# HGRN scores of levels 1 to 16 as 32-column tiles in one burst, and attention bursts in another order, in an inference step of a two-layer decoder

## The chip, the cores and the metric

One core of a Trainium2 chip runs the whole step. The metric is the device time of one execution in microseconds (us): 2629.91 before the change, the median of three runs (2628.09 to 2630.24).

## What is computed

The reference runs two groups of tokens through the same weights: a prompt of 256 tokens and 8 samples of 4 tokens, 288 columns in all. Layer 0 is an HGRN2 recurrence with 16 heads, layer 1 a sliding-window attention with sinks; each is followed by a SwiGLU FFN, and every sublayer stands between two RMS norms. What the change touches is the recurrence and the attention:

```
def step(S, inp):                      # gla_chunked, per head, float32
    qc, kc, vc, gc = inp
    b = jnp.cumsum(gc, axis=1)
    o_inter = jnp.einsum('bthk,bhkv->bthv', qc * jnp.exp(b), S)
    diff = b[:, :, None] - b[:, None, :]
    decay = jnp.exp(jnp.where(tril[None, :, :, None, None], diff, -jnp.inf))
    scores = jnp.einsum('bthk,bshk,btshk->btsh', qc, kc, decay)
    o_intra = jnp.einsum('btsh,bshv->bthv', scores, vc)
    b_last = b[:, -1]
    S_new = jnp.exp(b_last)[..., None] * S + jnp.einsum(
        'bshk,bshv->bhkv', kc * jnp.exp(b_last[:, None] - b), vc)
    return S_new, o_inter + o_intra
```

A score between a query at t and a key at s carries the product of the forget gates f between them, per element of the head's 128 dimensions. In the attention every query head takes the softmax of its scores over at most 128 keys and a sink, and multiplies the values.

## The kernel before

**Projections and ticks.** Activations lie transposed, 128 features by 288 tokens. `project` multiplies them by a weight matrix in steps of 128 rows. Weights come from memory as `raw`; ACT rounds them to `hi` (L219), DVE makes the rest `lo` (L220), and TensorE does three passes per block (`hi` and `lo` on the high part of the input, `hi` on the low part) into four accumulators of a tick: 12 passes of 288 columns. After each tick the function `tick` (L183) lets every launched generator run to its next `yield`. So a generator's matmuls stand between two ticks of a projection, in the order written; PE and ACT keep this order, DVE's is set by a scheduler. Everything small on PE shares three PSUM banks (`small`, L134).

**One HGRN head.** While head n + 1 is projected (16 ticks), the generator `recurrence` (L631) works on head n. It computes the decays in seven levels: at level B = 1, 2, 4, ... 64 a key in the first half of a block of 2B tokens meets the queries in the second half (the second 128 tokens run backwards, so there the halves change roles). Both have been multiplied by the gates up to the block's middle. Products of gates per block are in `Ts` (tile `tt`, L646).

- Step 1 starts the load of the sample state `s0` and makes `tt` and `qf` = q times f (L649). Four steps later comes the burst: scores of each token with itself and of the samples' own tokens, and the samples' queries with the state, all as tiles of 32 columns (L129 with `k`, `ksm`, `qsm`, `s0`).
- Then one step per level (`level`, L731): ACT merges the keys of both token halves into `km` (L678), DVE scales the keys (L705), PE multiplies 128 by 128, DVE scales the queries (L741) and copies the scores under a mask into `scp` (L742).
- Meanwhile values are transposed (L721, L722), spread per sample into `vb` (L748), the state is decayed into `sn` (L655). Then `state` (L778) adds the samples' new state, `ss` is stored, keys are transposed (L792), and the last steps make the output `po` and the prompt's final state.

After every second head, `gate_norm` (L578) normalizes two heads' outputs, in every second step, beside the next head's recurrence; its logarithm and exponential need another table on ACT (L300).

**Attention.** `prompt_heads` (L976) handles two heads ("par" 0 and 1, in rows 0 to 63 and 64 to 127 of the operands) in steps: scores (two banks), softmax, transposes (L996), values (L129 with `pt`, `vtok`). `sample_heads` (L1016) does the samples' eight sequences: four score bursts (par by half of the sequences; `kk`, `qs`, `kc`), one per tick, then four pairs of transposes (L1049, L1050) and four value bursts (`vnew`, `vc`).

**Fills.** Where a post-norm keeps PE from its next operand, `fill_time` (L142) runs 26, 24 and 19 matmuls of several shapes whose results nobody reads.

Of the kernel before, what the change touches and what calls it, by code (L numbers as in the profile page):

```python
# [11 lines left out]
F32 = mybir.dt.float32  # L12
F32R = mybir.dt.float32r
# [5 lines left out]
P = 128  # L19
# [19 lines left out]
NL = len(LEVELS)  # L39
FFN_PARTS = (16, 16, 12)  # L40
# [6 lines left out]
REC_DELAY = 4  # L47
# [67 lines left out]
def trunk(tc, I, O):  # L115
# [26 lines left out]
    def fill_time(kind, x):  # L142
        ps = small()
        y = strided(x, 0, [(1, 512)])
        b = y.bitcast(BF16)
        for n, rows, cols, src in (
            ((6, P, P, y), (6, P, TS, x), (4, P, P, x.rearrange("p (a b) -> p a b", a=2)), (6, P, P, x[:, :TP]), (4, P, P, x[:, :144])),
            ((6, 64, P, x), (6, P, 64, x), (6, P, P, strided(x, 0, [(2, NT)])), (6, P, P, strided(x, 2 * NT, [(1, NT)]))),
            ((8, P, P, b[:, :NT]), (6, P, P, b[:, :512]), (3, P, P, x.bitcast(F32))),
        )[kind]:  # L150
            out = ps[:cols, :src.free_size()] if len(src.shape) == 2 else ps[:cols, :NT].rearrange("p (a b) -> p a b", a=2)
            w = y.bitcast(src.dtype)[:rows, :cols]
            for _ in range(n):
                mm(out, w, src[:rows], True, True)

# [41 lines left out]
    fills = [0, 1, 2]  # L197
# [220 lines left out]
    def partial(pick, n, mix, first, norm=None, gcol=None, fill=None):  # L418
        add = None

        def each(m, acc):
# [7 lines left out]
            if m < 2:  # L429
                add = norm.square_one(dst)  # L430
                if m == 0:
                    gain(mix, gcol, 12)
            elif m == 2:
                norm.keep(dst)
            else:
                norm.flush(SPLIT)
                if fill is not None:
                    fill(PRE0)
                norm.tail(dst)
                if fill is not None:  # L440
                    fill(PRE1)
                else:
                    fill_time(fills.pop(0), pick(0)[0])
# [100 lines left out]
    with tc.tile_pool(name="hg", bufs=2) as hg:  # L544
        lmask = hg.tile([P, NL, P], U8, name="lmask", bufs=1)
# [3 lines left out]
        bmask = hg.tile([P, NB], F32, name="bmask", bufs=1)  # L549
        scores, scores_s = [], []  # L550
        for z in range(2):
            t = hg.tile([P, 2 * P], F32, name=f"sc{z}", bufs=1)
            nc.gpsimd.memset(t, 0.0)
            scores.append(t)
            t = hg.tile([P, TS], F32, name=f"scs{z}", bufs=1)
            nc.gpsimd.memset(t, 0.0)
            scores_s.append(t)

        def constants():
            wide = hg.tile([P, (NL + 1) * P + TS], mybir.dt.int32, tag="vb", name="wide", bufs=1)  # L560
# [6 lines left out]
            nc.vector.tensor_copy(lmask, wide[:, :NL * P].rearrange("p (l c) -> p l c", l=NL))  # L567
            yield
            nc.vector.tensor_copy(imask, wide[:TS, (NL + 1) * P:])
            nc.vector.tensor_copy(second, wide[:, NL * P:(NL + 1) * P])  # L570
# [41 lines left out]
        def evacuate(hd, accs, r):  # L612
            fg = hg.tile([P, NT], F32, tag="fg", name="fg", bufs=QB)
            q = hg.tile([P, NT], F32, tag="q", name="q", bufs=QB)
            gs = hg.tile([P, NT], F32, tag="gs", name="gs", bufs=3)
            k = hg.tile([P, NT], F32, tag="k", name="k", bufs=QB)
            v, s, s2 = work("v"), work("s"), work("s2")
# [9 lines left out]
            nc.vector.tensor_scalar(k, fg, -1.0, 1.0, op0=ALU.mult, op1=ALU.add)  # L627
            nc.vector.tensor_mul(gs, gs, s2)
            return q, fg, k, v, gs

        def recurrence(hd, delay, q, fg, k, v, gs):  # L631
            scp, scs = scores[hd % 2], scores_s[hd % 2]
            blk = scp.rearrange("p (a c) -> p a c", a=2)
            s0 = hg.tile([P, NB, P], F32, tag="s0", name="s0", bufs=1)
            (nc.gpsimd if hd else nc.sync).dma_start(s0, I["s0"][hd])
            rv = hg.tile([P, 4, TS], F32, tag="rep", name="rep", bufs=QB)
            nc.scalar.copy(rv, v[:, TP:NT].unsqueeze(1).broadcast_to([P, 4, TS]))
# [3 lines left out]
            for B in LEVELS:  # L641
# [6 lines left out]
            qf = hg.tile([P, NT], F32, tag="qf", name="qf", bufs=1)  # L648
            nc.vector.tensor_mul(qf, q, fg)  # L649
            t4 = Ts[2][:, 64:72]  # L650
            sn = hg.tile([P, NB, P], F32, tag="sn", name="sn", bufs=1)

            def decay(*bs):
                for b in bs:
                    nc.scalar.activation(sn[:, b, :], s0[:, b, :], AF.Identity, scale=t4[:, b:b + 1])  # L655

            yield
            ksm = hg.tile([P, 2, TS], F32, tag="ksm", name="ksm", bufs=1)
            qsm = hg.tile([P, 2, TS // 2], F32, tag="qsm", name="qsm", bufs=1)
            k2, q2 = [z[:, TP:NT].rearrange("p (j two) -> p j two", two=2) for z in (k, qf)]  # L660
            k4, q4 = [z[:, TP:NT].rearrange("p (j two b) -> p j two b", two=2, b=2) for z in (k, qf)]
            T1 = fg[:, TP:NT].rearrange("p (j two) -> p j two", two=2)
            T2 = Ts[1][:, P:P + TS // 2].rearrange("p (j two) -> p j two", two=2)
            nc.scalar.copy(ksm[:, 0, :], k[:, TP:NT])
            nc.scalar.copy(qsm[:, 0, :], q2[:, :, 1])
            nc.vector.tensor_mul(k2[:, :, 0], k2[:, :, 0], T1[:, :, 1])
            nc.vector.tensor_mul(q2[:, :, 1], q2[:, :, 1], T1[:, :, 0])
            nc.scalar.copy(ksm[:, 1, :], k[:, TP:NT])
            nc.scalar.copy(qsm[:, 1, :].rearrange("p (j b) -> p j b", b=2), q4[:, :, 1, :])
            nc.vector.tensor_mul(k4[:, :, 0, :], k4[:, :, 0, :], T2[:, :, 1:2].broadcast_to([P, NB, 2]))  # L670
            nc.vector.tensor_mul(q4[:, :, 1, :], q4[:, :, 1, :], T2[:, :, 0:1].broadcast_to([P, NB, 2]))

            kms = []

            def merge_k(li):
                B = LEVELS[li]
                km = hg.tile([P, P], F32, tag="km", name="km")
                nc.scalar.copy(km.rearrange("p (j s b) -> p j s b", s=2, b=B), strided(k, 0, [(2 * B, P // (2 * B)), (P + B, 2), (1, B)]))  # L678
                kms.append(km)

            for _ in range(delay - 1):
                yield
            merge_k(0)
            ps = small()
            for t in range(2):
                for g in range(4):
                    a = slice(t * P + g * TS, t * P + g * TS + TS)
                    mm(ps[TS * g:TS * (g + 1), t * TS:(t + 1) * TS], k[:, a], q[:, a], True, True)
            mm(ps[:TS, 2 * TS:3 * TS], ksm[:, 0, :], q[:, TP:NT], True, True)
            mm(ps[:TS, 3 * TS:3 * TS + 16], ksm[:, 0, :], qsm[:, 0, :], True, True)  # L690
            mm(ps[:TS, 3 * TS + 16:4 * TS], ksm[:, 1, :], qsm[:, 1, :], True, True)
            q = qf
            past = small()
            for g in range(4):
                mm(past[TS * g:TS * (g + 1), :2 * P].rearrange("p (b c) -> p b c", b=2), q[:, TP:NT], s0[:, 2 * g:2 * g + 2, :], True, True)
            own = hg.tile([P, 2, TS], F32, tag="own", name="own", bufs=1)
# [540 lines left out]
```

## Time and profile before

| | |
|---|---|
| three runs | 2628.09, 2629.91, 2630.24 us |
| the profiled execution | 2627.88 us |
| its span in the profile | 2626.1 us |
| granted clock of TensorE | 1.00 over the span |
| busy: PE, DVE, ACT | 2606.5, 1591.7, 1259.8 us |
| HGRN stage | up to about 550 us of the span |
| attention stage | about 1553 to 1700 us |

PE is TensorE's matmuls, PEld its weight loads, DVE VectorE, ACT ScalarE. A matmul of float32 operands appears as two passes, one of rounded operands as one. An instruction's duration reaches into the next one's: the distance from start to start says what it costs.

### The profile page before, as it was taken

To read this page: it belongs to the slowest core of one execution; us is meant where nothing else is said; L and a number is where in the kernel's file an instruction comes from. 1 tells how busy PE (TensorE), PEld (TensorE's weight loads), DVE (VectorE), ACT (ScalarE), POOL (GpSimd) and SP (SyncE) were. 2 spreads that over 40 slices of the span, in tenths; PEclk is the share of its full clock that TensorE was granted. 3 is DMA by queue.
4 is the path that set the end of the run, shared out by engine and by line. 5 is a ranking of instruction groups with operands and counts; after the bars stand their busy time and mean duration, and the time that the engine had idled before them with its cause. 6 is when DMAs were issued, how large, how long until landed. Compare 5 with 4: busy or idle time off the path is not lost.

```text
span 2626.1 us, 48851 instructions
## 1 busy us (share of the span) xinstructions
PE 2606.5 (99%) x20057; PEld 2565.5 (98%) x20058; DVE 1591.7 (61%) x2939; ACT 1259.8 (48%) x2217; POOL 34.2 (1%) x70
## 2 busy tenths in 40 slices
PE   9999999999999999999999999999999999999999
PEld 9999999999999999999999998899999999999998
DVE  8888888867654345544455787658544354544555
ACT  6666666655433334333334566656333343333343
POOL 0000000000000000000000000000000000000000
PEclk9999999999999999999999999999999999999999
DMA  6555555554545555455555553345455555555553
GB/s 225 178 167 168 163 165 169 165 161 148 180 155 178 166 169 163 159 177 166 164 166 169 165 158 105 99 159 166 156 178 166 166 165 161 175 165 167 162 161 123
DMA packets 119007, 428.03 MB, mean 163 GB/s; under 512 B 13792, under 2 KB 14112, under 8 KB 118784
## 3 DMA queue, kind: packets, MB, share of 16 engines
q1 hardware_dynamic: 112752, 404.49, 48.1%
q0 software_dynamic: 6032, 20.42, 2.3%
q8 instruction: 157, 2.57, 0.4%
q14 instruction: 66, 0.54, 0.1%
HBM read 412.74 MB, written 12.12 MB: 162 GB/s over the span
## 4 chain that ended last, share of the span: by engine, by line
PE 92%; DVE 5%; ACT 2%; issue 1%; DMA 0%; SPq 0%; DVEq 0%; ACTq 0%
PE acc L129 87%; PE pm L129 4%; DVE lo L220 1%; ACT hi L219 1%; DVE sc L742 1%; DVE qf L741 0%; DVE vb L748 0%; DVE k L705 0%; PE pm L996 0%; ACT y L594 0%; DMA raw<-w_in_in 0%; DVE v L760 0%; DVE mix L1129 0%; DVE yl L585 0%; ACT y L596 0%
## 5 line engine op out<-in xcount | busy, mean ns | idle before, releaser
L129 PE MATMUL acc<-xa,hi 128*128 128x288 f32 x12160 | 2476.5, 296 | 0.8 <-ACT xa L293 0.4
L129 PEld LDWEIGHTS acc<-xa,hi 128*128 128x128 f32 x12160 | 1971.5, 189 | 16.5 <-issue 14.2
L129 PE MATMUL acc<-xa,lo 128*128 128x288 f32 x6080 | 1791.6, 296 | 0.9 <-DVE lo L220 0.9
L220 DVE TENSOR_TENSOR lo<-raw,hi 128x1024 fp32r<-128x1024 f32 x759 | 919.0, 1224 | 747.7 <-ACT hi L219 746.9
L129 PEld LDWEIGHTS acc<-xa,lo 128*128 128x128 f32 x6080 | 1141.7, 188 | 2.0 <-DVE lo L220 1.1
L219 ACT CAST hi<-raw 128x1024 fp32r<-128x1024 f32 x759 | 784.1, 1048 | 715.8 <-PE acc L129 485.6
L474 ACT ACTIVATE f<-f 128x288 f32<-128x288 f32 x88 | 39.2, 445 | 203.9 <-DVE f L473 203.9
L473 DVE TENSOR_TENSOR f<-acc,rpre 128x288 f32<-128x288 f32 x84 | 38.4, 458 | 113.9 <-PE acc L129 113.9
L678 ACT COPY km<-k 128x128 f32<-128x128 f32 x112 | 34.8, 310 | 47.3 <-PE pm L129 23.8
L129 PE MATMUL pm<-qf,km 128*128 128x128 f32 x224 | 47.1, 292 | 8.6 <-ACT km L678 6.0
L293 ACT ACTIVATE xa<-h,gains 128x288 fp32r<-128x288 f32 x80 | 38.8, 527 | 31.8 <-DVE h L410 25.2
L129 PEld LDWEIGHTS pm<-qf,km 128*128 128x128 f32 x224 | 35.1, 189 | 13.4 <-ACT km L678 9.8
L742 DVE COPY_PREDICATED sc<-lmask,pm 128x128 f32<-128x128 uint8 x112 | 42.7, 381 | 0.9
L334 DVE TENSOR_TENSOR ss<-ss,sq 128x576 f32<-128x576 f32 x48 | 36.3, 757 | 10.3 <-ACT sq L333 8.6
L483 ACT CAST xa<-f 128x288 fp32r<-128x288 f32 x88 | 35.4, 434 | 14.0 <-DVE f L482 13.8
L655 ACT ACTIVATE sn<-s,tt 128x128 f32<-128x128 f32 x128 | 40.9, 392 | 0.0
L296 DVE SCALAR_TENSOR_TENSOR xa<-h,gains,xa 128x288 fp32r<-128x288 f32 x80 | 40.1, 517 | 0.4 <-ACT xa L293 0.4
L487 DVE TENSOR_TENSOR xa<-f,xa 128x288 fp32r<-128x288 f32 x88 | 36.6, 456 | 5.7
L741 DVE TENSOR_TENSOR qf<-qf,tt 128x128 f32<-128x128 f32 x96 | 27.7, 288 | 20.3 <-PE pm L129 19.9
L476 DVE TENSOR_TENSOR f<-acc,rpre 128x288 f32<-128x288 f32 x84 | 38.4, 457 | 0.0
L482 DVE TENSOR_TENSOR f<-f,f 128x288 f32<-128x288 f32 x88 | 36.1, 451 | 0.1
L452 DVE TENSOR_TENSOR mix<-acc,mix 128x288 f32<-128x288 f32 x56 | 22.2, 453 | 16.6 <-PE acc L129 16.6
(264 smaller groups left out, 1235.2 us busy)
## 6 DMA issues: line engine op xcount, KB each, us to landing
raw<-w_gu_in SPq DMA_DIRECT2D x352, 512.0 KB, 3.5
raw<-w_dn_in SPq DMA_DIRECT2D x176, 512.0 KB, 3.5
raw<-w_in_in SPq DMA_DIRECT2D x127, 512.0 KB, 3.6
raw<-w_oh_in SPq DMA_DIRECT2D x32, 512.0 KB, 3.7
raw<-w_q_in SPq DMA_DIRECT2D x32, 512.0 KB, 3.5
raw<-w_oa_in SPq DMA_DIRECT2D x32, 512.0 KB, 3.5
ss_out<-sn POOLq DMA_DIRECT2D x16, 512.0 KB, 6.1
s<-s_in POOLq DMA_DIRECT2D x15, 512.0 KB, 5.6
```

The costliest lines, as they stand in the source:

```text
L129: nc.tensor.matmul(out, lhsT, rhs, start=start, stop=stop, skip_group_check=True)
L219: nc.scalar.copy(hi, raw)
L220: lows.append(lambda: nc.vector.tensor_sub(lo, raw, hi.bitcast(F32)))
L293: nc.scalar.activation(xh, h[:, kt, :], AF.Identity, scale=g)
L296: nc.vector.scalar_tensor_tensor(xl, h[:, kt, :], g, xh.bitcast(F32), op0=ALU.mult, op1=ALU.subtract)
L334: return lambda: nc.vector.tensor_add(self.ss, self.ss, sq)
L473: nc.vector.tensor_mul(t1, accs[2 * a], r)
L474: nc.scalar.activation(t1, t1, AF.Silu)
L476: nc.vector.tensor_mul(t2, accs[2 * a + 1], r)
L487: nc.vector.tensor_sub(al, t2s[a], ah.bitcast(F32))
L655: nc.scalar.activation(sn[:, b, :], s0[:, b, :], AF.Identity, scale=t4[:, b:b + 1])
L742: nc.vector.copy_predicated(strided(scp, B, [(2 * B, n), (P - B, 2), (1, B)]), lmask[:, li].rearrange("p (j s b) -> p j s b", s=2, b=B), p ...
```

## The change

- Each head's keys and queries (after q times f) live in one tile `kq`, so that one DVE multiplication scales both for both token halves (`scale`). `pair` makes one level of `Ts` at a time.
- For levels 1 to 16 ACT keeps a merged copy of keys (`km`) and queries (`qm`) ahead of each scaling (`merge`). The scores of these five levels become 20 matmuls with 32 columns of keys and 32 of queries, in the one burst, which now comes at the ninth step. DVE copies them under five masks into `cs` (128 x 64) and multiplies `cs` out into `scp`. Levels 32 and 64 keep a full matmul each, one per step (`wide_scores`), and their copy comes a step later (`put`).
- The values' transposes come three steps before the burst, the keys' one step before. Three copies of the samples' keys and values go into the state's matmul in place of four. The state is decayed in place in `s0`. A head has 15 steps, it had 16.
- Prompt heads: the value matmuls of the two halves alternate. Sample heads: both halves of a score burst and of a value burst in one step; `vnew` and `pnew` have 128 rows, with zeros.
- `warm(30, ...)`, 30 matmuls of 288 columns, stands in place of `fill_time`.

```diff
+LOW = 5
+KQ = 4 * P + 2 * TS
-REC_DELAY = 4
+REC_DELAY = 2
...
-                    fill_time(fills.pop(0), pick(0)[0])
+                    warm(WARM, pick(0)[0])
...
+            def merge(li):
+                B = LEVELS[li]
+                km = hg.tile([P, P], F32, tag="km", name="km", bufs=LOW + 1)
+                nc.scalar.copy(km.rearrange("p (j s b) -> p j s b", s=2, b=B), strided(kq, 0, [(2 * B, P // (2 * B)), (3 * P + B, 2), (1, B)]))
+                kms.append(km)
+                if li < LOW:
+                    qm = hg.tile([P, P], F32, tag="qm", name="qm", bufs=LOW)
+                    nc.scalar.copy(qm.rearrange("p (s j b) -> p s j b", s=2, b=B), queries(li))
+                    qms.append(qm)
+            def scale(li):
+                B = LEVELS[li]
+                nc.vector.tensor_mul(halves(li), halves(li), strided(Ts[li], 1, [(-1, 2), (2, P // B), (0, B)]))
...
+            def wide_scores(li):
+                B = LEVELS[li]
+                n = P // (2 * B)
+                ps = small()
+                mm(ps[:, :P].rearrange("p (s j b) -> p s j b", s=2, b=B), kms.pop(0), queries(li), True, True)
+                scale(li)
...
+            merge(0)
+            yield
+            pair()
+            scale(0)
+            sample_scale(0)
+            merge(1)
+            yield
...
+            yield
+            pair()
+            scale(3)
+            merge(4)
+            yield
+            pair()
+            scale(4)
+            merge(5)
...
+            for li in range(LOW):
+                km, qm = kms.pop(0), qms.pop(0)
+                for g in range(4):
+                    a = slice(TS * g, TS * (g + 1))
+                    mm(ps[a, (2 + li) * TS:(3 + li) * TS].rearrange("p (s c) -> p s c", s=2), km[:, a], strided(qm, TS * g // 2, [(P // 2, 2), (1, TS // 2)]), True, True)
...
+            pair()
+            put = wide_scores(LOW)
+            merge(NL - 1)
+            nc.vector.tensor_tensor(scp.rearrange("p (t g c) -> p t g c", t=2, g=4), cs.unsqueeze(2).broadcast_to([P, 2, 4, TS]),
...
-            for par in range(2):
-                rows = slice(64 * par, 64 * par + 64)
-                hc = (2 * pair + par) * HD
-                mm(po[rows, :P], vtok[:, 0, hc:hc + HD], pt[:, par, 0, :], True, True)
-                mm(po[rows, P:TP], vtok[:, 1, hc:hc + HD], pt[:, par, 1, :], False, False)
-                mm(po[rows, P:TP], vtok[:, 2, hc:hc + HD], pt[:, par, 2, :], False, True)
+            for z in range(3):
+                for par in range(2):
+                    rows = slice(64 * par, 64 * par + 64)
+                    hc = (2 * pair + par) * HD
+                    mm(po[rows, P * (z > 0):P * (z > 0) + P], vtok[:, z, hc:hc + HD], pt[:, par, z, :], z == 0, z != 1)
...
+            for hb in range(2):
+                pss = [small() for _ in range(2)]
+                for ps, rows in zip(pss, halves):
+                    mm(ps[:, new[hb]], qv[rows, hb * P:(hb + 1) * P], kk[rows, pair, 3 * P:], True, True)
+                for bq in range(4):
+                    b = 4 * hb + bq
+                    for ps, rows in zip(pss, halves):
+                        mm(ps[32 * bq:32 * bq + 32, old[hb]], qv[rows, 32 * b:32 * b + 32], kc[rows, b, :], False, True)
...
+                for par, rows in enumerate(halves):
+                    hc = (2 * pair + par) * HD
+                    mm(po[rows, hb * P:(hb + 1) * P], vnew[:, hc:hc + HD], pnew[:, par * P:(par + 1) * P], hb == 0, False)
+                for bq in range(4):
+                    b = 4 * hb + bq
+                    for par, rows in enumerate(halves):
+                        mm(po[rows, 32 * b:32 * b + 32], vc[:, b, par * HD:(par + 1) * HD], pt[:, par * P + 32 * bq:par * P + 32 * bq + 32], False, True)
```

**PE, one HGRN head from the burst on, in a head with a gate norm.** Before (`pm` is a PSUM tile; `k`, `q` keys and queries, `s` the sample state, `km` merged keys; the projection's rows lie between, left out as "..."):

```order
L129 MATMUL pm<-q,k 32x32 [waits DVE_49]
L129 MATMUL pm<-q,k 32x32 x7
L129 MATMUL pm<-q,ksm 32x32 [waits Activation_49]
L129 MATMUL pm<-qsm,ksm 32x16 [waits Activation_49] x2
L129 MATMUL pm<-s_2232,qf 32x256 [waits DMASW1_49,DVE_49,PE_49]
L129 MATMUL pm<-s_2232,qf 32x256 x3
...
L721 MATMUL pm<-ident,v 128x128 x2
L722 MATMUL pm<-ident,rep 128x128
L129 MATMUL pm<-qf,km 128x128 [waits DVE_49]
```

and with the change:

```order
L132 MATMUL pm<-q,k_2260 32x32 [waits DVE_49]
L132 MATMUL pm<-q,k_2260 32x32 x7
L132 MATMUL pm<-qm,km 32x32 x16
L132 MATMUL pm<-qm,km 32x32 [waits Activation_49]
L132 MATMUL pm<-qm,km 32x32 x3
L132 MATMUL pm<-q,few 32x32
L132 MATMUL pm<-few 32x16 x2
L132 MATMUL pm<-s_2252,kq 32x256 [waits DMASW2_49,DVE_49]
L132 MATMUL pm<-s_2252,kq 32x256 x3
...
L132 MATMUL pm<-kq,km 128x128 [waits DVE_49]
...
L132 MATMUL pm<-kq,km 128x128 [waits Activation_49]
```

The 20 matmuls with `qm` have come into the burst. Behind it seven ticks held a level each (of the before one is shown); two are left, and the second waits for ACT's merge.

**DVE, from the burst to the scaling of level 32 and 64, in a head without a gate norm.** Before, per level (`sc` is `scp`):

```order
L705 TENSOR_TENSOR k<-k,tt 128x2x32x2 [waits Activation_49]
L741 TENSOR_TENSOR qf<-qf,tt 128x2x32x2 [waits PE_49]
L742 COPY_PREDICATED sc_120<-lmask,pm 128x32x2x2
L705 TENSOR_TENSOR k<-k,tt 128x2x16x4 [waits Activation_49]
L741 TENSOR_TENSOR qf<-qf,tt 128x2x16x4 [waits PE_49]
```

and with the change:

```order
L765 TENSOR_TENSOR cs<-pm,eyes 128x64 [waits PE_49]
L769 COPY_PREDICATED cs<-lmask,pm 128x2x16 [waits DVE_49]
L769 COPY_PREDICATED cs<-lmask,pm 128x2x8x2 [waits DVE_49]
L779 COPY_PREDICATED every<-second,pm 128x128 [waits Activation_49]
L769 COPY_PREDICATED cs<-lmask,pm 128x2x4x4 [waits DVE_49]
L769 COPY_PREDICATED cs<-lmask,pm 128x2x2x8 [waits DVE_49]
L772 COPY_PREDICATED scs<-imask,pm 32x32
L784 TENSOR_TENSOR scp<-cs,bmask 128x256 [waits DVE_49]
L673 TENSOR_TENSOR kq<-kq,tt 128x2x4x32 [waits PE_49]
L692 COPY_PREDICATED scp<-wmask,pm 128x2x2x32
L673 TENSOR_TENSOR kq<-kq,tt 128x2x2x64 [waits PE_49]
```

Three operations per level have become one scaling (L673), which for levels 1 to 16 stands ahead of the burst; the copies of the burst's scores now stand ahead of the scaling of level 32.

**PE, a score burst of the samples beside a prompt head's scores.** Before:

```order
L129 MATMUL pm<-kk,q 128x128 [waits DVE_49,PE_49]
L129 MATMUL pm<-kk,q 128x256
L129 MATMUL pm<-kk,qs 128x32 [waits DVE_49,Activation_49]
L129 MATMUL pm<-kc,qs 32x128 [waits DMASW7_49]
L129 MATMUL pm<-kc,qs 32x128 x3
```

and with the change:

```order
L132 MATMUL pm<-kk,q 128x128 [waits DVE_49,PE_49]
L132 MATMUL pm<-kk,q 128x256
L132 MATMUL pm<-kk,qs 128x32 [waits DVE_49,Activation_49]
L132 MATMUL pm<-kk,qs 128x32 [waits DVE_49]
L132 MATMUL pm<-kc,qs 32x128 [waits DMASW7_49]
L132 MATMUL pm<-kc,qs 32x128 x7
```

The burst holds both halves and waits twice for DVE, once per PSUM bank.

## Rows read from the trace of the kernel before

**Rows 1.** The page, busy time and share; and the chain by engine:

```profile
PE 2606.5 (99%) x20057; PEld 2565.5 (98%) x20058; DVE 1591.7 (61%) x2939; ACT 1259.8 (48%) x2217; POOL 34.2 (1%) x70
...
PE 92%; DVE 5%; ACT 2%; issue 1%; DMA 0%; SPq 0%; DVEq 0%; ACTq 0%
```

**Rows 2.** Windows: stretch, length, PE, PEld, DVE, ACT, POOL busy, clock, DMA, GB/s:

```profile
700.00:1300.00 600.00, 600.00 (x4540) 600.00 (x4540) 285.59 (x333) 226.36 (x269) 0.00 (x0) 1.00 0.52 166
104.75:137.58 32.83, 31.85 (x262) 30.70 (x261) 29.45 (x77) 23.18 (x52) 1.61 (x3) 1.00 0.47 160
137.58:168.89 31.31, 31.07 (x259) 30.16 (x258) 23.96 (x65) 17.05 (x42) 1.61 (x3) 1.00 0.55 175
```

**Rows 3.** Timeline of PE, one head: start, length in us, line, operands, count:

```profile
201.67 0.33 PE L129 MATMUL pm<-q,k 128*32 128x32 f32 x16
201.82 0.23 PE L129 MATMUL pm<-q,ksm 128*32 128x32 f32 x2
...
202.01 0.60 PE L129 MATMUL pm<-s,qf 128*32 128x256 f32 x5
202.54 0.40 PE L129 MATMUL acc<-xa,hi 128*128 128x288 f32 x1
...
208.36 0.38 PE L129 MATMUL pm<-qf,km 128*128 128x128 f32 x2
...
210.17 0.39 PE L129 MATMUL pm<-qf,km 128*128 128x128 f32 x2
...
212.37 0.46 PE L129 MATMUL pm<-qf,km 128*128 128x128 f32 x2 [0.24 <-DVE qf L741]
```

**Rows 4.** The chain in a head with a gate norm: start, length, engine:

```profile
111.81 0.45 ACT L300
...
114.03 0.68 ACT y L596
...
115.15 0.49 PE pm L129 x2
```

**Rows 5.** Groups of instructions: busy us, mean ns of one, idle before:

```profile
L220 DVE TENSOR_TENSOR lo<-raw,hi 128x1024 fp32r<-128x1024 f32 x759 | 919.0, 1224 | 747.7 <-ACT hi L219 746.9
...
L678 ACT COPY km<-k 128x128 f32<-128x128 f32 x112 | 34.8, 310 | 47.3 <-PE pm L129 23.8 <-DVE k L705 23.5
...
L649 DVE TENSOR_TENSOR qf<-q,fg 128x288 f32<-128x288 f32 x16 | 7.3, 455 | 0.0
```

**Rows 6.** Timeline of DVE, the evacuation ahead of that burst:

```profile
194.82 0.45 DVE L618 TENSOR_TENSOR q<-acc,rpre 128x288 f32<-128x288 f32 x1
...
197.72 0.31 DVE L627 TENSOR_SCALAR k<-fg 128x288 f32<-128x288 f32 x1
```

**Rows 7.** Timeline of PE in the attention stage:

```profile
1570.54 1.15 PE L129 MATMUL pm<-pt,vtok 128*64 128x128 f32 x12
...
1575.43 0.93 PE L129 MATMUL pm<-kk,q 64*128 64x128 f32 x8
...
1587.18 0.41 PE L129 MATMUL pm<-kk,qs 64*128 64x32 f32 x2
...
1587.87 0.40 PE L129 MATMUL acc<-xa,hi 128*128 128x288 f32 x1
...
1614.28 0.43 PE L129 MATMUL pm<-pts,vnew 32*64 32x128 f32 x2
...
1615.22 0.33 PE L1049 MATMUL pm<-ident,ssm 128*128 128x128 f32 x1
...
1618.49 1.55 PE L129 MATMUL pm<-kk,q 64*128 64x128 f32 x8
```

**Rows 8.** Timeline of PE, the first fill:

```profile
625.09 4.09 PE L129 MATMUL pm<-xa 128*128 128x512 f32 x26
```

**Rows 9.** DMA issues: queue, count, KB each, us to landing:

```profile
ss_out<-sn POOLq DMA_DIRECT2D x16, 512.0 KB, 6.1
s<-s_in POOLq DMA_DIRECT2D x15, 512.0 KB, 5.6
```

More of the change, by code (lines that the diff above doesn't have):

```diff
@@ L140, in warm @@
             mm(ps[:, :rhs.shape[-1]], rhs[:, :P], rhs, True, True)
[L142 to L154, printed above, removed]
     def work(name):
@@ L640, in recurrence, with pair @@
             toff = 0
-            for B in LEVELS:
+            def pair():
+                nonlocal toff
+                B = LEVELS[len(Ts) - 1]
                 nb = (NT if B < 4 else TP) // (2 * B)
@@ L659, in recurrence @@
[L659 to L681, printed above, removed]
+                    nc.scalar.activation(s0[:, b, :], s0[:, b, :], AF.Identity, scale=t4[:, b:b + 1])
+            kms, qms = [], []
+            def halves(li):
+                B = LEVELS[li]
+                return strided(kq, 0, [(2 * P + B, 2), (2 * B, P // B), (1, B)])
@@ new lines, in queries @@
+            def queries(li):
+                B = LEVELS[li]
+                return strided(kq, P, [(P + B, 2), (2 * B, P // (2 * B)), (1, B)])
+            def merge(li):
[7 more added lines that the diff above has]
+                    qms.append(qm)
@@ L682, in recurrence @@
+            merge(0)
+            yield
+            pair()
[4 more added lines that the diff above has]
+            pair()
+            scale(1)
+            sample_scale(1)
+            merge(2)
+            yield
+            for _ in range(delay):
                 yield
-            merge_k(0)
+            pair()
+            scale(2)
+            merge(3)
+            rk = hg.tile([P, 3, TS], F32, tag="rep", name="rep", bufs=QB)
             ps = small()
@@ new lines, in recurrence @@
+            merge(5)
+            k3ps = small()
+            nc.tensor.transpose(k3ps[:3 * TS, :P], rk.rearrange("p a b -> p (a b)"), ident)
+            k3 = hg.tile([3 * TS, P], F32R, tag="k3", name="k3", bufs=1)
+            nc.scalar.copy(k3, k3ps[:3 * TS, :P])
+            nc.vector.tensor_sub(k3[2 * TS:3 * TS], k3ps[2 * TS:3 * TS, :P], k3[2 * TS:3 * TS].bitcast(F32))
+            yield
+            pair()
+            ps, past = small(), small()
+            for t in range(2):
+                for g in range(4):
+                    a = t * P + g * TS
+                    mm(ps[TS * g:TS * (g + 1), t * TS:(t + 1) * TS], k0[:, a:a + TS], q[:, a:a + TS], True, True)
@@ L778, in state @@
+            spread(0, NB // 2)
+            decay(*range(NB // 2))
+            yield
+            put()
+            put = wide_scores(NL - 1)
+            spread(NB // 2, NB)
+            decay(*range(NB // 2, NB))
             def state(half):
@@ L795, in recurrence @@
             yield
+            state(1)
+            nc.gpsimd.dma_start(O["ss"][hd], s0)
             smid = hg.tile([P, P], F32, tag="smid", name="smid", bufs=1)
@@ L1182, in shape_constants @@
     i = (np.arange(P) % 4)[:, None]
-    sm = np.zeros((P, 2, 160), np.float32)
-    for hb in range(2):
-        b = 4 * hb + np.arange(P)[:, None] // 32
-        n = np.arange(TS)[None, :]
-        new = (n // 4 == b) & (n % 4 <= i)
-        sm[:, hb] = np.where(np.concatenate([k > i, new], 1), 0.0, NEG)
-    c["smask"] = sm
+    b = np.arange(P)[:, None] // 32
+    n = np.arange(TS)[None, :]
+    new = [(n // 4 == 4 * hb + b) & (n % 4 <= i) for hb in range(2)]
+    c["smask"] = np.where(np.concatenate([new[0], k > i, new[1]], 1), 0.0, NEG).astype(np.float32)
     return c
```

293 lines of the change are left out of this document (132 added, 161 removed).

## The prediction

> **What bounds the kernel now.** I read the page's busy shares and its chain of waits first. TensorE is busy for 99% of the span and carries 92% of the chain [rows 1]: whatever lies on PE's queue is paid, and work elsewhere is free unless PE waits for it. Next the windows. In a stretch of plain projections 600 us hold 4540 matmuls [rows 2], 0.132 us each, at a granted clock of 1.00. A tick of the program (four accumulators, three passes each) is thus 12 x 0.132 = 1.58 us, and whatever stands between two ticks adds its own time. Two HGRN heads take 32.83 + 31.31 = 64.14 us [rows 2], against 32 ticks x 1.58 = 50.7 us of projection: 13.4 us per pair are recurrence and waits, and this is where the change works. The longer of the two also carries the gate norm of the pair before it.
>
> The timeline of one head shows the pieces [rows 3]. The burst of 32-column tiles starts at 201.67 and the projection is back at 202.54. After it each level's matmul of full width stands alone between two ticks: from 208.36 to 210.17 is 1.81 us, so one level costs 1.81 - 1.58 = 0.23 us. From 210.17 to 212.37 is 2.20: the same 0.23 and 0.39 of waiting, since the next level needs the queries that DVE scales after the last one. In a head with the gate norm the wait is longer: ACT's table load at 111.81 and what follows hold back the merged keys, and PE's level matmul starts only at 115.15 [rows 4].
>
> **The change, part by part.** The sum is made against the profiled execution, 2627.88 us, which is 2.0 us under the median of the three runs.
>
> *Levels as tiles.* Five of seven level matmuls leave their ticks: 5 x 0.23 = 1.15 us per head. Twenty 32-column matmuls join the burst, two passes each, 40 passes. The 16 passes of the same form that stand there now start between 201.67 and 201.82 [rows 3], 0.0094 us each, since four column groups run side by side; 40 x 0.0094 = 0.38 us. Net -0.77 us, times 16 heads: **-12.3 us**. The bounds of a pass are 0.009 and the 0.11 of a full-width pass (0.23 / 2). I take the low end, because those rows are the same shape in the same place; the high end is a rival below. The transposes of values and keys only change ticks, and the two levels left keep a matmul each: nothing.
>
> *Waits.* Now: 0.39 us in a plain head; in one with the gate norm 32.83 - 31.31 = 1.52 more, of which its four 288-column matmuls are 4 x 0.132 = 0.53, so 1.38 us of waiting. With nine heads of the first kind and seven of the second: 9 x 0.39 + 7 x 1.38 = 13.2 us. After the change PE meets the keys once, in the burst, eight ticks after the head begins. Now DVE's evacuation starts at 194.82 [rows 6] and the head's burst at 201.67 [rows 3], 6.85 us later and four ticks after the head's first step; with the change it stands four ticks and 0.44 us of transposes (0.33 for three passes and 0.11 for one) further on: 13.6 us. What must fit: the evacuation from 194.82 to 198.03, 3.2 us [rows 6]; new keys and queries at most 2 x 0.46 [rows 5], 0.9; five rounds of one scaling (256 columns, at most 0.46, the 288-column product) and two merges on ACT (0.31 each) [rows 5], 1.08 each, 5.4; and about three splits of weights (1.22 each [rows 5]) that DVE takes between, 3.7. Together 13.2 us if none overlap, and splits and merges do. So plain heads wait for nothing. In the gate-norm heads the table load, two logarithms and an exponential lie ahead of the last merge on ACT, 2.9 us from 111.81 to 114.71 [rows 4], of which I let 0.2 show at the burst, 0.4 at the 64-level (its keys are merged one tick after the 32-level's scaling, behind the six copies that DVE makes of the burst) and 0.5 where the state's matmul wants one of three PSUM banks that those copies still hold: 1.1 us. 7 x 1.1 = 7.7 us left of 13.2: **-5.5 us**. Bounds: nothing left (-13.2), or a full 1 us in every head (16 us, +2.8).
>
> *What covers the rest.* DVE loses three operations of 128 columns per level and gains one of 256; ACT gains five merged-query copies of 0.31. In a head with the gate norm DVE is busy for 29.45 of 32.83 us and ACT for 23.18 [rows 2]: both still fit. The state is decayed in place, so the next head's load waits for this head's store on POOL's queue: 6.1 + 5.6 us [rows 9]. The store can go three ticks before the head ends, the load is wanted at the ninth step: 12 ticks, 19 us. Nothing, unless DVE is over 5 us late.
>
> *Attention, prompt heads.* The 12 value passes take 1.15 us from first start to last end [rows 7], because six of one half stand before six of the other. Alternating, six pairs: five steps of 0.11 and the last pass of 0.27, at best 0.82; the first pass has been slower than the others, so I take 0.87. 16 x 0.28 = **-4.5 us** (bounds 0 and -5.3).
>
> *Attention, sample heads.* A score burst runs from 1587.18 to 1587.87 [rows 7], 0.69 us. Eight become four, each with both halves, which lie in different rows of the array as the halves of the prompt's scores do: -4 x 0.69 = -2.8. A value burst, 1614.28 to 1615.22, 0.94 us; eight become four: -3.8. New waits: a score burst now wants two PSUM banks beside the two of a prompt head's scores, and there are three. Such a collision is in the trace: the scores that take 0.93 us alone take 1.55 beside a value burst [rows 7], 0.6 more. Four of them: +2.4. Together **-4.2 us** (bounds 0 and -6.6).
>
> *Filling matmuls.* 26 take 4.09 us from 625.09 [rows 8]; 30 of 0.132 take 3.96. Nothing: the norm's chain, which they cover, still ends after them; were it shorter, 30 in place of 26, 24 and 19 would cost 21 x 0.132 = 2.8 us at most.
>
> Sum: -12.3 - 5.5 - 4.5 - 4.2 = -26.5; 2627.9 - 26.5 = 2601.4. I forecast **2602 us**, about 2604 if the run falls where the median does.
>
> **Rivals.** *The waits come back.* The scalings and merges are five hand-overs between DVE and ACT, both in order; if each meets a weight split, the burst is late. For it: the gate-norm heads above, only 0.4 us of slack in the plain ones where nothing overlaps. Against: the merged keys were late before because each level waited for PE too. Price: 1 us in all 16 heads is 16 us where I have 7.7: 2610; 1.5 us: 2618. Chance 0.2.
>
> *The long burst does not keep its pace, and the kernel becomes slower.* The burst grows from 30 passes to 70, and no row shows more than 30 short passes in a row. If the passes that are added start every p us, the price over my term is 16 x 40 x (p - 0.009). It eats the 26.5 us at p = 0.05. At the full-width pace of 0.11 it is +65 us: 2666. The six sample passes in one column group start between 201.82 and 202.01 [rows 3], 0.03 apart; at that pace, the four groups not side by side, it is +13 us: 2615. For it: nothing has been seen past 30. Against: 25 of those 30 have started by 202.01, in 0.34 us, with no slowing. Chance of slower 0.04, of the middle 0.09.
>
> The Trainium skill's page "TensorE: Matmul & The Clock Gate", section "Wait — 56ns, not 53.3ns?", says that with hardware decode off the sequencer spends about 62 ns on a matmul, which binds once the array's work is shorter. By it, as an estimate, the 40 passes would take 2.5 us per head and the kernel about 2636 us. No run so far shows it.
>
> *The change gives more:* the banks come free in time and no head waits. 2602 - 7.7 - 2.4 = 2592, and 2587 if the lone ticks that vanish were dearer than 0.23. Chance 0.13.
>
> *It does not do what it says:* the halves of the value passes do not run side by side, as half of them do not now. 2602 + 4.5 + 2.8 = 2609. This lies in the forecast's own range.
>
> **How the numbers follow.** Forecast (2594 to 2610) 0.51, more 0.13, waits back 0.2, slow burst in its middle form 0.09, a little of everything down to no gain 0.03, slower 0.04. The range from 2587 to 2618 leaves out about 0.15. A measurement of this kernel tells some 0.2% (5.3 us) from no change: faster 0.93, same 0.03, slower 0.04.
>
> **What would show it.** In the profile after: full-width level matmuls fall from 224 passes to 64 and 640 passes of 32 columns appear; the burst lasts about 1.25 us from first start to the projection's return; two heads take about 62 us; idle PE time shows in heads with the gate norm alone, before the burst and the 64-level; 12 value passes last under 0.9 us. It is wrong if the burst lasts over 2 us, if plain heads wait for merged keys, or if the scaling row on DVE ends PE's idle time in most heads.

## The result and the profile after

The changed kernel takes **2600.56 us**, the median of four runs (2599.99 to 2601.87), against 2629.4 us before: a ratio of 0.9894 with a 95% interval of 0.9881 to 0.9906. The forecast was 2602, and about 2604 for the median. The profiled execution took 2601.87 us, 26.0 us less than that of before, where the sum had 26.5. The sum is right, and the terms under it are not: the HGRN stage gave 5.4 us more than its terms, and the attention 5.9 us less.

The page's busy shares and the chain by engine, as in [rows 1]:

```profile
PE 2583.6 (99%) x20558; PEld 2547.7 (98%) x20558; DVE 1575.3 (61%) x2813; ACT 1262.9 (49%) x2241; POOL 34.4 (1%) x70
...
PE 93%; DVE 5%; ACT 1%; issue 1%; DMA 0%; SPq 0%; DVEq 0%
```

PE still bounds everything; ACT's share of the chain has fallen from 2% to 1%. The filling matmuls of the three post-norms are landmarks that cut the span into stages. Their rows in PE's timeline, of the changed kernel:

```profile
601.85 4.20 PE L132 MATMUL pm<-xa 128*128 128x288 f32 x30
...
1446.01 4.20 PE L132 MATMUL pm<-xa 128*128 128x288 f32 x30
...
1741.36 4.21 PE L132 MATMUL pm<-xa 128*128 128x288 f32 x30
```

and the second and third of the kernel before (the first is in [rows 8]):

```profile
1469.42 4.30 PE L129 MATMUL pm<-xa 64*128 64x288 f32 x24
...
1767.55 3.89 PE L129 MATMUL pm<-xa 128*128 128x288 bf16 x19
```

| stretch | before | after | difference | the prediction's terms |
|---|---|---|---|---|
| start to the first fill (HGRN) | 625.09 | 601.85 | -23.2 | -12.3 - 5.5 = -17.8 |
| first to second fill | 844.33 | 844.16 | -0.2 | 0 |
| second to third fill (attention) | 298.13 | 295.35 | -2.8 | -4.5 - 4.2 = -8.7 |
| third fill to the end | 858.55 | 858.74 | +0.2 | 0 |

**HGRN.** Windows of two heads, from burst to burst (columns as in [rows 2]):

```profile
107.72:138.63 30.91, 30.68 (x288) 29.38 (x287) 28.34 (x68) 20.80 (x51) 1.61 (x3) 1.00 0.53 173
138.63:169.12 30.49, 30.49 (x292) 29.77 (x291) 23.08 (x58) 19.84 (x48) 1.61 (x3) 1.00 0.55 175
```

The pair takes 61.40 us where it took 64.14 [rows 2]. PE's timeline in a plain head, from the burst to the state's matmul:

```profile
199.95 0.33 PE L132 MATMUL pm<-q,k 128*32 128x32 f32 x16
200.09 0.52 PE L132 MATMUL pm<-qm,km 128*32 128x32 f32 x38
...
201.15 0.40 PE L132 MATMUL acc<-xa,hi 128*128 128x288 f32 x1
...
202.84 0.38 PE L132 MATMUL pm<-kq,km 128*128 128x128 f32 x2
...
206.51 0.39 PE L132 MATMUL pm<-vb,k 96*128 96x512 f32 x1
...
206.88 0.38 PE L132 MATMUL acc<-xa,hi 128*128 128x288 f32 x1
```

and the same places in a head with a gate norm:

```profile
107.72 0.33 PE L132 MATMUL pm<-q,k 128*32 128x32 f32 x16
...
108.92 0.40 PE L132 MATMUL acc<-xa,hi 128*128 128x288 f32 x1
...
110.84 0.49 PE L132 MATMUL pm<-kq,km 128*128 128x128 f32 x2
...
115.05 0.51 PE L132 MATMUL pm<-vb,k 96*128 96x512 f32 x1 [0.15 <-DVE scp L692]
...
115.53 0.38 PE L132 MATMUL acc<-xa,hi 128*128 128x288 f32 x1
```

The burst lasts 201.15 - 199.95 = 1.20 us where it lasted 0.87 [rows 3], in both kinds of head: with its 40 new passes it is 0.33 us longer, 8.3 ns a pass. From the burst's end to the projection's return after the state, the plain head takes 206.88 - 201.15 = 5.73 us, the other one 115.53 - 108.92 = 6.61: 0.88 us of waits are left in a head with a gate norm, and none at its burst.

**Attention.** PE's timeline in the changed kernel: twelve value passes, and the place where the samples' second transposes meet a prompt head's scores.

```profile
1564.03 0.88 PE L132 MATMUL pm<-pt,vtok 128*64 128x128 f32 x12
...
1586.45 0.61 PE L132 MATMUL pm<-pts,vc 128*64 128x32 f32 x16
1588.60 0.44 PE L1068 MATMUL pm<-ident,ssm 128*128 128x128 f32 x2 [1.54 <-DVE s L1006]
...
1591.18 0.68 PE L132 MATMUL acc<-xa,hi 128*128 128x288 f32 x2
1591.66 0.44 PE L132 MATMUL acc<-xa,lo 128*128 128x288 f32 x1
1591.90 0.44 PE L132 MATMUL acc<-xa,hi 128*128 128x288 f32 x1
```

The value passes are down from 1.15 us [rows 7] to 0.88. But PE idles 1.54 us for a PSUM bank that DVE still reads (L1006), and the projection behind that runs at 0.24 us a pass (1591.66 to 1591.90) in place of 0.132. The waits of PE in the stage, in all, times, longest:

```profile
PE pm L132 <- DVE s L1006: 2.5, 2, 1.6
PE pm L1068 <- DVE s L1006: 1.5, 1, 1.5
```

and windows, with the granted clock third from the end:

```profile
1584.00:1590.00 6.00, 4.28 (x43) 3.53 (x42) 4.70 (x19) 3.83 (x15) 0.00 (x0) 0.91 0.39 118
1590.00:1596.00 6.00, 6.00 (x59) 5.68 (x59) 1.48 (x10) 2.77 (x13) 0.55 (x1) 0.81 0.32 91
1638.00:1644.00 6.00, 5.49 (x47) 4.64 (x48) 2.77 (x17) 0.97 (x4) 0.00 (x0) 0.72 0.26 90
```

The granted clock fell twice from 1.00 to its lower level, 1.2 GHz, each time after an idle PE (1.54 and 1.60 us). Each window lacks its length times what is missing to 1.00: 6 x (0.09 + 0.19 + 0.28) = 3.4 us in all.

### The profile page after: what moved, and what is told of

Same layout as the page of the kernel before. It is cut to its first block, busy times and chain, and to the rows that moved or that the text cites. A ratio compares the mean times of both kernels' runs of the same rounds, so it can differ in the third digit from the quotient of the medians.

```text
span 2600.1 us, 49708 instructions
## 1 busy us (share of the span) xinstructions
PE 2583.6 (99%) x20558; PEld 2547.7 (98%) x20558; DVE 1575.3 (61%) x2813; ACT 1262.9 (49%) x2241; POOL 34.4 (1%) x70
## 4 chain that ended last, share of the span: by engine, by line
PE 93%; DVE 5%; ACT 1%; issue 1%; DMA 0%; SPq 0%; DVEq 0%
PE acc L132 88%; PE pm L132 4%; DVE lo L208 1%; ACT hi L207 1%; DMA raw<-w_in_in 0%; PE pm L1016 0%; DVE t L923 0%; DVE mix L1152 0%; DVE t L919 0%; DVE vb L729 0%; DVE kq L673 0%; DVE cs L769 0%; DVE t L920 0%; DVE y L591 0%; DVE q L964 0%
## 5 line engine op out<-in xcount | busy, mean ns | idle before, releaser
L664 ACT COPY km<-kq 128x128 f32<-128x128 f32 x112 | 34.4, 307 | 48.0 <-DVE kq L673 28.2
L673 DVE TENSOR_TENSOR kq<-kq,tt 128x256 f32<-128x256 f32 x96 | 40.6, 423 | 8.9 <-ACT qm L668 5.9
L649 ACT ACTIVATE s<-s,tt 128x128 f32<-128x128 f32 x128 | 39.3, 389 | 0.0
L798 DVE TENSOR_TENSOR s<-pm,s 128x512 f32<-128x512 f32 x32 | 22.0, 688 | 11.3 <-ACT s L649 10.1
L438 ACT COPY mix<-acc 128x288 f32<-128x288 f32 x32 | 12.7, 400 | 32.9 <-PE acc L132 32.8
L981 ACT ACTIVATE s<-s,mx 128x128 f32<-128x128 f32 x64 | 24.8, 390 | 0.9 <-DVE mx L975 0.8
```

The lines of the kernel that those rows point to most:

```text
L649: nc.scalar.activation(s0[:, b, :], s0[:, b, :], AF.Identity, scale=t4[:, b:b + 1])
L673: nc.vector.tensor_mul(halves(li), halves(li), strided(Ts[li], 1, [(-1, 2), (2, P // B), (0, B)]))
```

## The experiments

Ten kernels, each a small edit of the changed one. "A" in the expectations is the reading above, "B" mostly the prediction's. Executions of the same HGRN code reach the first fill up to 1.9 us apart (601.71 to 603.60 us in the first three kernels below). Nearly all of that is the clock: in the slowest (`shift`) the granted clock from 12 to 18 us is 0.72, where the others have 1.00: 6 x 0.28 = 1.7 us. So totals are medians, and where time went is read between landmarks.

**1. The samples' bursts as before (`sample_old`).** One half per step again, in scores and values:

```diff
-            for hb in range(2):
-                pss = [small() for _ in range(2)]
+            for par in range(2):
+                for hb in range(2):
+                    ps = small()
...
```

> The changed kernel, with the samples' score and value bursts of the attention put back to eight and eight of one half each, as before the change. Theory A (from the trace of the changed kernel): the paired bursts cost more than they save, because PE waits for PSUM banks beside a prompt head's scores (4.9 us over four places) and the granted clock falls twice after such a wait (mean-clock deficits of 1.7 us each). The attention stage became 3.1 us shorter where the alternating value passes alone give 4.3, so this part cost 1.2: about 2599.4 us, and no window under a granted clock of 1.00 in the attention stage. Theory B (the prediction's term): the paired bursts are worth 4.2 us, so undoing them gives about 2604.8 us.

Measured: 2601.0 us (2600.8 to 2601.81), as the changed kernel within the runs' spread. Its second and third fill:

```profile
1445.83 4.21 PE L132 MATMUL pm<-xa 128*128 128x288 f32 x30
...
1740.71 4.21 PE L132 MATMUL pm<-xa 128*128 128x288 f32 x30
```

The attention takes 294.88 us: 0.5 less than with the paired bursts. The clock stays at 1.00 and PE no longer waits for L1006. B's 4.2 us of gain are not there. A's loss of 1.2 us is not shown either: the kernels of experiments 4 to 7 and 10 run the changed kernel's attention as it is, and its time depends on the clock. Two of them (`twice`, `delay3`) lose the clock twice, as the changed kernel does, and take 295.44 and 295.16 us. Three (`column`, `delay1`, `level16`) have the same two waits of PE but lose it only behind the second, and take 293.91, 293.60 and 293.60. In `column` the projection keeps its pace of 0.13 us a pass behind the first wait:

```profile
1594.32 0.44 PE L1068 MATMUL pm<-ident,ssm 128*128 128x128 f32 x2 [1.54 <-DVE s L1006]
...
1595.34 0.29 PE L132 MATMUL acc<-xa,lo 128*128 128x288 f32 x1
1595.47 0.44 PE L132 MATMUL acc<-xa,hi 128*128 128x288 f32 x2
```

So the paired bursts as built lie between 0.6 us dearer and 1.3 us cheaper than the old ones: worth about nothing.

**2. The samples moved by a tick (`shift`).**

```diff
-S0D = 10
+S0D = 11
-H2, H3, S3 = 9, 5, 4
+H2, H3, S3 = 9, 5, 3
-NDV, TURN, SSY = 2, 2, 2
+NDV, TURN, SSY = 2, 2, 3
```

> The changed kernel with the two sample generators moved by a tick each way (the first starts one tick later, the second one earlier, and one more tick stands between scores and values), so that no score burst and no transposes of the samples share a tick with a prompt head's scores, which take two of the three PSUM banks. Theory A: the four waits for banks (4.9 us) go, and with them the two falls of the clock (3.4 us): about 2592.4 us, clock 1.00 in the whole attention stage. Rival 1: the waits come from three banks for too many tiles wherever the bursts stand; they only move, and the time stays about 2600 us. Rival 2: the waits go but the clock falls anyway because the bursts of short passes themselves count as little work: about 2596 us.

Measured: **2595.67 us** (2594.45 to 2596.72; ratio to before 0.9874, 0.9859 to 0.9889). Its second and third fill in PE's timeline:

```profile
1447.70 4.21 PE L132 MATMUL pm<-xa 128*128 128x288 f32 x30
...
1736.19 4.22 PE L132 MATMUL pm<-xa 128*128 128x288 f32 x30
```

and a window over all four bursts of the samples:

```profile
1560.00:1680.00 120.00, 119.12 (x1073) 105.36 (x1072) 94.05 (x362) 84.18 (x286) 1.10 (x2) 1.00 0.39 119
```

The attention takes 288.49 us, 6.9 less than in the changed kernel, at a clock of 1.00 throughout; the waits for L1006 are gone. Both rivals fall: the waits came from the place of the bursts, and the same bursts at another place do not lower the clock. Against experiment 1 the paired bursts, rightly placed, are worth 294.88 - 288.49 = 6.4 us; what the old bursts would take at the new place was not run.

**3. The value passes as before (`prompt_old`).**

```diff
-            for z in range(3):
-                for par in range(2):
+            for par in range(2):
+                for z in range(3):
```

> The changed kernel with the value passes of the prompt heads in the order of before: six of one half, then six of the other. Theory A: side-by-side halves are worth 0.27 us per head (1.27 to 1.00 us of added time per tick): 16 x 0.27 = 4.3 us slower, about 2604.9 us. Rival: the passes are bound by something that the order does not change, and the shorter time came from elsewhere in the tick: about 2600.6 us.

Measured: 2604.07 us (2601.66 to 2605.05), 3.5 slower; from its second fill (1445.92) to its third (1744.56) 298.64 us, 3.3 more. The halves do run side by side. The missing us of the 4.3 goes to waits behind the shorter ticks: in the changed kernel the prompt's transposes at 1624.89 us cost 0.4 us more than here, and two ticks beside the samples (from 1581.87 and 1584.80) 0.5 more. Both kernels lose the clock twice in this stage.

**4. The low levels twice (`twice`).**

```diff
-                for g in range(4):
+                for g in (0, 1, 2, 3, 0, 1, 2, 3):
```

> The changed kernel with the twenty matmuls of levels 1 to 16 in each burst issued twice (the second time over the same place with the same operands), so that a burst holds 110 short passes in place of 70. It prices 40 more passes. Theory A: they start every 0.0085 to 0.0094 us, as the first 40 did (burst 1.40 us over the pitch where it was 1.06): 16 x 0.34 to 0.38 = 5.4 to 6.0 us slower, about 2606.3 us. Rival 1: the pace lasts only as long as instructions stand ready in PE's queue; past 70 it falls to the 0.03 us of one column group alone: 16 x 40 x 0.03 = 19 us, about 2620 us. Rival 2, by the Trainium skill's figure of about 62 ns per matmul: 16 x 40 x 0.062 = 40 us, about 2640 us.

Measured: 2610.5 us (2608.54 to 2611.68). PE's timeline, level 64 in a head with a gate norm, and then the burst of a plain head:

```profile
114.95 0.49 PE L132 MATMUL pm<-kq,km 128*128 128x128 f32 x2 [1.12 <-ACT km L664]
...
140.35 0.33 PE L132 MATMUL pm<-q,k 128*32 128x32 f32 x16
140.50 0.85 PE L132 MATMUL pm<-qm,km 128*32 128x32 f32 x78
...
141.91 0.40 PE L132 MATMUL acc<-xa,hi 128*128 128x288 f32 x1
```

The burst is 1.56 us long, 0.36 more; over all 16 heads PE's time around it grows by 0.33 us each, 8.3 ns a pass again, in a burst of 110 passes. Rivals 1 and 2 fall. Most of the rest of the 9.9 us is a wait that A did not foresee. DVE's order of work is made anew for every build. In the changed kernel's first head with a gate norm it reads

```
L769 COPY_PREDICATED cs<-lmask,pm 128x2x8x2
L673 TENSOR_TENSOR kq<-kq,tt 128x2x4x32
L769 COPY_PREDICATED cs<-lmask,pm 128x2x4x4
L208 TENSOR_TENSOR lo<-raw,hi 128x1024
```

and in this one

```
L769 COPY_PREDICATED cs<-lmask,pm 128x2x8x2
L208 TENSOR_TENSOR lo<-raw,hi 128x1024
L769 COPY_PREDICATED cs<-lmask,pm 128x2x4x4
L673 TENSOR_TENSOR kq<-kq,tt 128x2x4x32
```

The scaling of level 32 (L673) has come behind a weight split of 1.22 us, and the keys merged after it are late for level 64 in all seven heads with a gate norm: 7.8 us of idle PE. Other waits behind the burst shrink by it: from the burst's end to the projection's return after the state such a head takes 7.10 us where the changed kernel takes 6.61, so that 7 x 0.5 = 3.5 us are left as the price.

**5. The levels of one column group in a row (`column`).**

```diff
-            for li in range(LOW):
-                km, qm = kms.pop(0), qms.pop(0)
-                for g in range(4):
+            for g in range(4):
+                for li, (km, qm) in enumerate(lows5):
```

> The changed kernel with the twenty low-level matmuls of each burst in another order: the five levels of one column group in a row, then the next group, in place of the four groups of one level in a row. The passes, operands and waits are the same. Theory A (the burst is short because neighbours lie in different column groups and run side by side): 40 passes at the 0.03 us of one column group alone, in place of 0.0083: 16 x 40 x 0.022 = 14 us slower, about 2614.5 us, and the burst some 0.9 us longer. Rival: the sequencer, not the array, sets the pace of these passes, so the order does not matter: about 2600.6 us.

Measured: 2607.04 us (2604.54 to 2609.3). Its burst, PE's timeline:

```profile
139.95 0.33 PE L132 MATMUL pm<-q,k 128*32 128x32 f32 x16
140.10 1.04 PE L132 MATMUL pm<-qm,km 128*32 128x32 f32 x37
```

Nothing but the order differs, and the `qm` passes take 0.52 us more (1.04 for 37, where 38 took 0.52): the side-by-side start is the order's doing, and the rival falls. The price is half of the 14 us expected, for two reasons: the passes lost 13 ns each, not 22, and behind a burst half a us longer PE waits less: from the burst's end to the return after the state a head with a gate norm takes 6.08 us in place of 6.61, 3.7 us in all seven. That DVE used the time to catch up is the likely reason.

**6. The burst a tick earlier (`delay1`).**

```diff
-REC_DELAY = 2
+REC_DELAY = 1
```

> The changed kernel with one step less ahead of the burst, so that the burst stands one tick (1.58 us and the transposes ahead of it) earlier in every head. Theory A (from the trace of the changed kernel: in a plain head the last merge ends 2.4 us before the burst, in a head with a gate norm at the burst itself): plain heads stay without a wait, the seven with a gate norm wait 1 to 1.6 us more: 7 to 11 us slower, about 2609 us. Theory B (the prediction's sum, 13.2 us of work in 13.6 us in every head): every head waits about 1.2 us: 19 us slower, about 2620 us. Rival: DVE and ACT catch up because the steps are only ordered by the tick, not timed by it: 2600 us.

Measured: 2606.18 us (2605.2 to 2609.2). The longest of PE's waits in the stage:

```profile
PE pm L132 <- DVE yl L575: 2.8, 7, 0.4
```

Plain heads show no wait though their burst stands a tick earlier, so theory B, the prediction's 13.2 us of work in 13.6, falls: they had over 1.6 us to spare. In the seven heads with a gate norm PE loses time at two places. The gate norm's own sums now come before DVE has the squares (L575): they hold PE 1.57 us where they held it 0.53. And the burst waits in its middle, where A put it:

```profile
109.93 0.87 PE L132 MATMUL pm<-qm,km 128*32 128x32 f32 x40
```

That makes the burst 1.56 us long in place of 1.20. Together the two cost 1.4 us, A's size; but behind the burst 0.8 us less is lost (5.83 us in place of 6.61), which A had not seen, so a pair of heads ends up 0.6 us longer.

**7. The burst a tick later (`delay3`).**

```diff
-REC_DELAY = 2
+REC_DELAY = 3
```

> The changed kernel with one more step ahead of the burst; the parts of the gate norm move by one tick with it. Theory A (DVE comes late to the burst in a head with a gate norm): a tick more lets it catch up, and the 0.9 us of waits that such a head still has behind the burst go: 7 x 0.9 = 6 us faster, about 2594.5 us. Theory B (the waits follow the burst wherever it stands, since they are for PSUM banks and for the copies out of them): about 2600.6 us. Rival: the head now ends one tick later and meets the next head's evacuation: slower, some 16 x 0.5 = 8 us, about 2609 us.

Measured: 2596.74 us (2595.92 to 2599.2), 3.8 less. The state's matmul waits no longer, and the profile lists no wait of PE in the stage; about 0.3 us a head is left at level 64. That is A, at two thirds of its size: DVE's lateness was most of the wait. (This execution, like that of `delay1`, has the clock of 0.72 from 12 to 18 us.)

**8. Levels 32 and 64 in the bank of the samples' queries, with the shift (`best`).**

```diff
-                ps = small()
...
-            put = wide_scores(LOW)
+            put = wide_scores(LOW, past[:, 2 * P:3 * P])
-            put = wide_scores(NL - 1)
+            put = wide_scores(NL - 1, past[:, 3 * P:])
```

> The kernel with the shifted sample generators, and the scores of levels 32 and 64 written to the unused half of the PSUM bank that holds the samples' queries times the state, so that they take no bank of their own. Theory A: the wait ahead of level 32 (0.33 us, for the bank of the transposed samples' keys) and the one ahead of the state's matmul (0.43 us, for the bank of level 32) go in the seven heads with a gate norm: 7 x 0.76 = 5.3 us less than the shifted kernel's 2595.7: about 2590.4 us. Rival: the banks are only the last of several things that are late, and DVE's order of work puts the same wait at the transposes of the keys, which need the scaling of level 64: about 2595.7 us.

Measured: 2620.34 us (2619.2 to 2622.78), a miss by 30 us. PE's waits in the HGRN stage:

```profile
PE pm L132 <- ACT s L649: 12.9, 7, 1.9
PE pm L132 <- DVE every L778: 4.0, 8, 0.5
```

PE's timeline at level 64 of a head with a gate norm:

```profile
116.00 0.46 PE L132 MATMUL pm<-kq,km 128*128 128x128 f32 x2 [1.82 <-ACT s L649]
```

and DVE's timeline, the copy of level 32's scores:

```profile
115.55 0.30 DVE L691 COPY_PREDICATED scp<-wmask,pm 128x128 f32<-128x128 uint8 x1
```

The wait is put down to ACT's decay, but in the program level 64's matmul has gained a wait for DVE: it writes the tile that DVE's copy of level 32 still reads, though other columns of it, and the copy stands behind the burst's own copies and ends at 115.85. ACT's decays end within 0.03 us of it, so the trace alone does not part the two; but in the changed kernel the same matmul starts at 112.83 while the decays run on to 115.13, and the edit adds no wait for them. The Trainium skill's page "PSUM — Partial Sum Buffer", section "PSUM bank collisions raise a hardware error", asks for such a guard by bank and quadrant of 32 partitions, not by address. Both operations here use all partitions of the bank, and the trace shows the guard's price. Saving a bank by sharing one joins two waits that had been apart.

The waits are not the whole miss. In six of the seven heads the granted clock falls to its lower level behind them, 0.72 for example from 504 to 510 us; the windows of 6 us around these places lack 10.1 us in all. Behind the first such wait, the 1.82 us above, the clock stays at 1.00.

**9. The two that helped, together (`best2`).** The edits of experiments 2 and 7.

> The shifted sample generators and the later burst together, neither with any other edit. Theory A: the two act in different stages, so the gains add up: 4.9 us of the first and 3.8 us of the second below the changed kernel's 2600.6: about 2591.8 us. Rival: one of the two gains was a matter of where DVE's order of work fell in that build, and it is not there in this one: 2595 to 2597 us.

Measured: **2590.65 us** (2589.98 to 2591.68; ratio to before 0.9855, 0.9841 to 0.987): 38 us faster than before and 9.9 faster than the change. The gains add up, as A said (2591.8).

**10. Level 16 back out of the burst (`level16`).**

```diff
-LOW = 5
+LOW = 4
...
+            merge(NL - 1)
...
+            yield
+            put()
+            put = wide_scores(NL - 1)
```

> The changed kernel with level 16 taken out of the burst again: a full-width matmul in a tick of its own, ahead of levels 32 and 64, so that a head has one more step. Four levels are tiles in place of five. Theory A (a level's price is its passes alone): 0.223 us for the tick against 8 passes of 0.0083 us: 16 x 0.157 = 2.5 us slower, about 2603.1 us. Theory B (each full-width level is also one more place where PE meets keys that DVE and ACT have just scaled and merged): another 0.4 to 0.9 us in each of the seven heads with a gate norm, 3 to 6 us: 2606 to 2609 us. Rival: PE has slack for it, since the same tick also gives DVE 1.6 us more: 2600 us or less.

Measured: 2606.86 us (2606.31 to 2608.27), 6.3 slower: B's size, at a third place again.

```profile
PE pm L132 <- DVE ms L585: 5.9, 7, 0.9
```

In the heads with a gate norm the burst waits for the banks of the gate norm's sums, which DVE (L585) has not read yet; in the plain ones the second full-width level waits 0.2 us for its keys. One level more as a full matmul thus costs 0.4 us a head, 0.16 of it in passes: it is the meeting with DVE and ACT that is dear, not the matmul.

## Why the prediction was right

- **Levels as tiles, -12.3.** Right, a little small. The burst's new passes cost 0.33 us where I had 0.38, and experiment 4 gives the same 8.3 ns. Of the 2.74 us that a pair saves, 0.77 a head and the waits below account for 2.4; the rest I can't split between passes and the waits of before.
- **Waits, -5.5.** Too small. In heads with a gate norm 0.88 us is left where I had 1.1: 6.2 us in place of 7.7. It lies at level 32, level 64 and the state; the 0.2 that I put at the burst is not there. And the first heads, which my rows did not show, had longer waits before, as one row of that kernel's waits says:

```profile
PE pm L129 <- ACT qsm L669: 1.2, 1, 1.2
```

  Eight pairs at 2.74 are 21.9 us, and 1.3 more fell in the first ones. Together the two terms are 23.2 where I had 17.8.
- **The slack of plain heads.** The conclusion (no wait) was right, the step to it wrong: 13.2 us of 13.6 added up work that overlaps. By experiment 6 at least a tick is free.
- **Prompt value passes, -4.5.** The 12 passes take 0.88 us where I had 0.87, and the term is worth 3.3 to 3.5 (experiment 3), since waits behind them took up a part. The kernel before and `sample_old`, both at a clock of 1.00, give the same: 298.13 - 294.88 = 3.25.
- **Sample heads, -4.2.** The step that failed. "Four of them: +2.4" was a price of 0.6 us for a meeting at a bank; the meetings cost up to 1.6, and the idle PE then lost its clock, some 1.7 us each time, for which the sum had no term. By experiments 1 and 2 the term is +0.5 in this execution (-1.3 where the clock fell once) and -6.4 without meetings, near my bound of -6.6.
- **Fills, 0.** Right: from the first to the second 0.2 us less.
- **Rivals.** The slow burst is out (experiment 4). The Trainium skill's page "TensorE: Matmul & The Clock Gate", section "Wait — 56ns, not 53.3ns?", has some 62 ns per matmul with hardware decode off and a floor of about 25 ns from start to start with either decode. The measurement differs and decides: with four column groups in turn a pass takes 8.3 ns here and a matmul of two passes 17, so that neither binds. The waits came back only where an edit brought them (experiments 4, 8 and 10).
- **What was to show it.** Full-width level passes from 224 to 64, and 640 of 32 columns: yes. Burst 1.25 us: 1.20. Two heads about 62: 61.4. Idle PE in HGRN in heads with the gate norm alone: yes, though not ahead of the burst.

So the total was right by luck: two errors of some 5.5 us met with opposite signs. The main mechanism, levels as short passes at 8 to 9 ns and fewer waits, was right in itself.

## What to carry to other kernels

Before a burst is made wider, lay it beside what shares its tick and count the PSUM banks that both hold: the same bursts were worth 6.4 us at one tick and about nothing at another, and moving them took three constants. A small matmul put between other work is paid mostly where it meets keys or banks that another engine has just handled, so batching pays by the meetings it saves; and where work on the other engines is late, a start one tick later can be faster. If a scheduler orders an engine anew for each build, read that order too before an edit's price is put down to the edit.

## What the runs showed of the hardware

- 32-column passes that go round the four column groups keep a pace of 8.3 ns over 80 added passes (experiment 4); the same 40 passes with the five levels of one group in a row take 13 ns more each (experiment 5).
- TensorE's granted clock fell from 1.00 to its lower level, 1.2 GHz, behind idle stretches of 1.5 to 1.9 us, but not behind every one. With the same waits of 1.54 and 1.60 us in the attention it fell behind both in the changed kernel, `prompt_old`, `twice` and `delay3`, and behind the second alone in `column`, `delay1` and `level16`. Each fall cost about 1.7 us. The kernels without these waits (experiments 1 and 2) kept 1.00 in the same stage. What decides between the two is not shown.
